# Two token groups run side by side under a static list schedule: an eight-core hybrid decoder step

## The chip, the cores and the metric

The kernel runs on all 8 cores of one Trainium2 chip (cores 0 to 3 are die 0, cores 4 to 7 die 1). Each core takes one prompt sequence and 16 decode sequences, and no core talks to another. The time is device microseconds (us) of the slowest core. PE is the matmul engine, ACT the scalar engine, DVE the vector engine, POOL the GpSimd engine, and SP the engine that only issues transfers here.

The runs fall in two states. In the fast one the two dies agree (kernel before: clocks of 0.92 to 0.95 on every core, and the dies' median spans within 0.7%); in the slow one the cores of one die show a lower granted PE clock and the time is longer.

## The reference, cut to what matters

Two layers; each token's activations `x` are 1024 wide. This is one layer:

```python
hn = rmsnorm(x, norm_in)
u_a, b_a, c_a, g_a, x_b, g_b, m_a, m_b = split(hn @ w_in)      # 8 x 1024 columns
y_a = b_a * conv3(c_a * u_a) * silu(g_a)                       # branch A
xc  = conv4(x_b) + bias                                        # branch B
r, gi = sigmoid(xc @ w_r), sigmoid(xc @ w_i)                   # block-diagonal, 64 x 64
a = exp(-8 * r * softplus(-lam))
h[t] = a[t] * h[t-1] + sqrt(1 - a[t]**2) * gi[t] * xc[t]       # scan over time
y_b = h * silu(g_b)
m = sigmoid(m_a) * (y_a @ w_a_out) + sigmoid(m_b) * (y_b @ w_b_out)
x = x + m @ w_o
x = x + (p @ w_pe) * sigmoid(rmsnorm(x, norm_pe) @ w_pg)
```

A final RMSNorm follows the second layer. Per core there are 2112 token columns: 2048 of the prompt and 64 of the decode group. The convolutions and the scan run along time, so a tile of columns needs the last few columns of the tile before it.

Below, the **A phase** of a token group is everything up to `y_a` and `y_b`; it is heavy on ACT and DVE (77% and 84% busy in the first row of the stretches below). The **B phase** is the merge, `w_o`, the second norm and the gate; it is mostly PE (100% in the second row, with ACT at 17% and DVE at 32%).

## The kernel before

Features lie on the 128 partitions and tokens on the free dimension. The tokens are handled as two groups, one wholly after the other, since the kernel's on-chip arrays hold `x`, `hn`, `ya`, `yb` and `mg` of one group at a time:

```python
def tiles_of(g):
    if g == 0:
        return [("p", 512, 0, 0), ("m", 512, 512, 512)]
    return [("p", 384, 0, 1024), ("p", 384, 384, 1408), ("p", 320, 768, 1792)]
...
for g in range(2):
    # load x of this group
    for l in range(L):
        norm_phase(g, V_NIN + l * 8, hn)
        for j in range(KC):                      # the A phase, 8 column blocks
            for ti, tile in enumerate(tl):
                c = ab_front(ui, g, l, j, ti, tile)
                if pend is not None:
                    ab_back(pend)                # gates and scan, one unit late
                pend = c
        ab_back(pend)
        # the B phase: mg_unit, wo_unit, norm_phase, gt_unit, each for 8 blocks
    norm_phase(g, V_NF, None, final=True, after_tile=store_tile)
```

Each engine's instruction stream is in program order, with semaphore waits computed from reads and writes. Weights are fetched by POOL into a ring of five slots, one 1024 x 128 column block per transfer:

```python
def wsrc_cols(wl, c0):
    return wl[:, c0:c0 + 128].rearrange("(k p) n -> p k n", p=128)
```

The sources are fp32, so that reads runs of 128 x 4 = 512 bytes; they are cast to bf16 on the way. SiLU is written with Tanh, the function that the sigmoids use as well, plus one vector instruction; the factors 0.5 are folded into other instructions:

```python
act(s2[:, 0:n], psum[b_gb][:, 0:n], AF.Tanh, [("ps", b_gb)], [s2k], scale=0.5)
...
stt(s2[:, 0:n], s2[:, 0:n], 1.0, psum[b_gb][:, 0:n], ALU.add, ALU.mult, [s2k, ("ps", b_gb)], [s2k])
```

## Time and profile before

The median of the first three runs is 1877.32 us, but two of these three are slow (1877.32 and 1899.26); the fast one is 1824.2. The profiled execution is a fast one with a span of 1819.5 us.

From the page of the kernel before: busy time and share of the span by engine; then the span in 40 slices, with a digit for tenths busy; then the weight queue (packets, MB, share of the 16 DMA engines' time); then the engines' shares in the chain that ended last; then one costly group (busy us, mean ns, idle time ahead of it).

```profile
PE 1565.0 (86%) x8200; PEld 809.0 (44%) x8200; DVE 1148.9 (63%) x2162; ACT 969.6 (53%) x1677; POOL 596.5 (33%) x715
...
PE   3989889988999889987198888999889889799985
...
PEclk9999999988999999988599999999889999999987
...
q0 software_dynamic: 415008, 105.48, 65.2%
...
PE 44%; DVE 22%; ACT 15%; issue 8%; DMA 7%; POOL 3%; DVEq 0%; ACTq 0%; POOLq 0%; SPq 0%
...
L226 ACT ACT_TABLE_LOAD x177 | 227.1, 1283 | 11.3 <-PE ps L250 7.2
```

PE is the busiest engine, but 1819.5 - 1565.0 = 254.5 us of the span it does nothing, and it makes up only 44% of the chain. The digits show where: many 8s, and a hole (7, 1) in the middle, where the first group ends and the second has to be loaded. The clock digits fall with it, to 5 (0.50 in the fourth row below).

Busy time by stretch says what each stage is worth. The columns are the stretch, its length, then busy time (and instructions) of PE, PEld, DVE, ACT and POOL, then granted clock, DMA share and GB/s.

```profile
75.00:264.00 189.00, 165.64 (x737) 71.63 (x736) 158.69 (x293) 144.63 (x227) 88.84 (x111) 0.97 0.74 64
264.00:376.00 112.00, 112.00 (x521) 50.67 (x520) 35.85 (x52) 18.63 (x31) 23.27 (x28) 1.00 0.74 66
376.00:440.00 64.00, 56.71 (x237) 23.32 (x236) 37.46 (x56) 22.26 (x37) 23.55 (x29) 0.92 0.75 67
860.00:912.00 52.00, 10.63 (x28) 3.12 (x29) 12.38 (x22) 12.84 (x30) 0.00 (x0) 0.50 0.88 192
```

The first row is an A phase: 737 matmuls in 189 us, 256 ns each, with DVE busy 84% and ACT 77%. The second is a merge: 521 matmuls in 112 us, 215 ns each, with DVE a third busy and ACT a sixth. So in one stage the vector work holds PE up, and in the next PE holds the others up. The fourth row is the hole between the groups.

The waits of PE name the same places (total us, times, longest):

```profile
PE ps L365 <- ACT wk_sq L226: 92.1, 21, 38.8
PE ps L250 <- DVE wk_xc L240: 81.3, 44, 3.0
PE ps L250 <- DMA wslot<-w_in: 17.4, 6, 7.2
```

The first is the norms (PE sums squares that ACT makes), with a single wait of 38.8 us between the groups. The second is the A phase. PE hardly ever waits for weights, though their queue takes 65% of the DMA engines.

### The profile page before, as it was taken

The numbers are of one execution on the slowest core, as the hardware profiler recorded it, in microseconds if no ns is written. First come the engines' busy times: TensorE is split into PE (matmuls) and PEld (weight loads), VectorE is DVE, ScalarE is ACT, GpSimd is POOL, SyncE is SP. The second block draws the span as 40 slices with busy tenths as digits, with TensorE's granted clock in tenths as the row PEclk, the third lists the DMA queues.
The fourth block names the chain that finished last, engine by engine and source line by source line (L and its number), as shares of the span: only waits on it lengthen the run. The fifth ranks groups of instructions, "written<-read, shape, count | busy, mean of one in ns | idle before, by whom it ended". The sixth has DMA issues, their size and how long they took to land.

```text
span 1819.5 us, 23966 instructions; the slowest of 8 cores (1808.0 to 1819.5 us)
## 1 busy us (share of the span) xinstructions
PE 1565.0 (86%) x8200; PEld 809.0 (44%) x8200; DVE 1148.9 (63%) x2162; ACT 969.6 (53%) x1677; POOL 596.5 (33%) x715
## 2 busy tenths in 40 slices
PE   3989889988999889987198888999889889799985
PEld 0333334433433334432054555566445445466642
DVE  3688872346888863356188888433678888833365
ACT  3577761134687751134278888411357888831144
POOL 5244451024345451023023444411233435340120
PEclk9999999988999999988599999999889999999987
DMA  9866979169676889269825739863594465894353
GB/s 171 81 50 56 79 66 103 18 60 86 60 63 53 75 72 97 25 59 97 203 20 51 69 37 90 72 60 30 54 101 39 43 63 51 77 90 44 38 52 117
DMA packets 426390, 126.05 MB, mean 69 GB/s; under 512 B 412832, under 2 KB 421792, under 8 KB 426272
## 3 DMA queue, kind: packets, MB, share of 16 engines
q0 software_dynamic: 415008, 105.48, 65.2%
q1 hardware_dynamic: 11264, 19.04, 3.6%
q8 instruction: 70, 1.15, 0.2%
q14 instruction: 48, 0.39, 0.1%
HBM read 220.44 MB, written 9.49 MB: 126 GB/s over the span
## 4 chain that ended last, share of the span: by engine, by line
PE 44%; DVE 22%; ACT 15%; issue 8%; DMA 7%; POOL 3%; DVEq 0%; ACTq 0%; POOLq 0%; SPq 0%
PE ps L250 42%; DVE wk_xc L240 9%; ACT wk_th L226 5%; DMA wslot<-w_in 5%; DVE wk_h L533 4%; DVE wk_ti L229 2%; PE ps L365 2%; ACT wk_a L226 2%; DVE x L240 2%; ACT wk_ti L226 1%; ACT wk_tr L226 1%; DMA yT<-x 1%; DVE hn L240 1%; DVE wk_tg L240 1%; ACT wk_xc L226 1%
## 5 line engine op out<-in xcount | busy, mean ns | idle before, releaser
L250 PE MATMUL ps<-hn,wslot 128*128 128x512 bf16 (+2 forms) x5760 | 1119.3, 350 | 115.5 <-DVE wk_xc L240 81.3
L250 PEld LDWEIGHTS ps<-hn,wslot 128*128 128x128 bf16 x5760 | 568.8, 100 | 624.3 <-issue 189.1
L226 ACT ACTIVATE wk_tg<-ps 128x512 f32<-128x512 f32 (+2 forms) x240 | 125.0, 521 | 281.8 <-PE ps L250 199.0
L315 POOL DMA_DIRECT2D wslot<-w_in x256 | 228.8, 908 | 119.7 <-PE ps L250 100.9
L240 DVE SCALAR_TENSOR_TENSOR wk_tg<-wk_tg,ps 128x512 f32<-128x512 f32 (+2 forms) x240 | 141.8, 591 | 157.1 <-PE ps L250 114.2
L226 ACT ACT_TABLE_LOAD x177 | 227.1, 1283 | 11.3 <-PE ps L250 7.2
L229 POOL TENSOR_TENSOR ya<-wk_cv,wk_tg 128x512 bf16<-128x512 f32 (+2 forms) x80 | 106.9, 1336 | 342.8 <-DVE wk_cv L240 342.8
L226 ACT ACTIVATE wk_sq<-x 128x512 bf16<-128x512 f32 (+2 forms) x200 | 93.2, 541 | 162.3 <-PE ps L365 75.4
L226 ACT ACTIVATE wk_cv<-ps 128x320 f32<-128x320 f32 (+1 forms) x160 | 83.3, 521 | 179.5 <-PE ps L250 179.5
L365 PE MATMUL ps<-wk_sq,ones 128*128 128x512 bf16 (+2 forms) x200 | 81.8, 461 | 106.9 <-ACT wk_sq L226 92.1
L240 DVE SCALAR_TENSOR_TENSOR wk_xc<-ps,vecs_sb,wk_xc 128x511 f32<-128x511 f32 (+8 forms) x240 | 152.6, 636 | 9.9 <-ACT sop_sb L419 3.9
L240 DVE SCALAR_TENSOR_TENSOR hn<-x,vecs_sb,wk_xc 128x512 bf16<-128x512 f32 (+2 forms) x160 | 92.9, 652 | 92.2 <-ACT wk_xc L226 92.2
L240 DVE SCALAR_TENSOR_TENSOR wk_cv<-wk_cv,ps 128x512 f32<-128x512 f32 (+2 forms) x80 | 47.5, 594 | 163.8 <-PE ps L250 163.8
L250 PE MATMUL ps<-ya,wslot 128*128 128x512 bf16 (+2 forms) x640 | 130.3, 347 | 0.0
L250 PE MATMUL ps<-yb,wslot 128*128 128x512 bf16 (+2 forms) x640 | 127.3, 342 | 2.9 <-POOL yb L229 2.9
L315 POOL DMA_DIRECT2D wslot<-w_o x32 | 28.1, 877 | 289.9 <-PE ps L250 289.9
L229 POOL TENSOR_TENSOR yb<-wk_h,wk_s 128x512 bf16<-128x512 f32 (+2 forms) x80 | 86.4, 1080 | 108.2 <-DVE wk_h L533 108.2
L229 DVE TENSOR_TENSOR wk_ti<-wk_th,wk_ti 128x512 f32<-128x512 f32 (+2 forms) x80 | 57.7, 721 | 93.1 <-ACT wk_th L226 93.1
L250 PE MATMUL ps<-mg,wslot 128*128 128x512 bf16 (+2 forms) x640 | 115.0, 342 | 0.0
L240 DVE SCALAR_TENSOR_TENSOR wk_cv<-wk_cu,dv,wk_cv 128x384 f32<-128x384 f32 (+3 forms) x160 | 102.4, 640 | 2.8
L365 PEld LDWEIGHTS ps<-wk_sq,ones 128*128 128x128 bf16 x200 | 20.4, 102 | 167.2 <-issue 165.9
L226 ACT ACTIVATE wk_th<-wk_th 128x512 f32<-128x512 f32 (+2 forms) x160 | 88.8, 555 | 3.4
(71 smaller groups left out, 1487.6 us busy)
## 6 DMA issues: line engine op xcount, KB each, us to landing
wslot<-w_in POOLq DMA_DIRECT2D x256, 256.0 KB, 11.4
wslot<-w_a_out POOLq DMA_DIRECT2D x32, 256.0 KB, 14.4
wslot<-w_b_out POOLq DMA_DIRECT2D x32, 256.0 KB, 17.7
wslot<-w_o POOLq DMA_DIRECT2D x32, 256.0 KB, 4.5
wslot<-w_pg POOLq DMA_DIRECT2D x32, 256.0 KB, 4.5
x<-xin SPq DMA_DIRECT2D x2, 2048.0 KB, 20.1
yT<-x SPq DMA_DIRECT2D x2, 2048.0 KB, 23.4
x<-xin SPq DMA_DIRECT2D x2, 1536.0 KB, 14.4
```

Source lines behind the costliest of these rows:

```text
L226: P.op("act", lambda e: e.activation(out=out, in_=in_, func=func, **kw), reads, writes)
L229: P.op(eng, lambda e: e.tensor_tensor(out=out, in0=in0, in1=in1, op=op), reads, writes)
L240: P.op("dve", lambda e: e.scalar_tensor_tensor(out=out, in0=in0, scalar=scalar, in1=in1, op0=op0, op1=op1), reads, writes)
L250: ins = e.matmul(out=psum[bk][:, 0:n], lhsT=lh, rhs=rh, start=(i == 0), stop=(i == len(pairs) - 1))
L315: pending.append((ui_, (lambda e, s=src, d=dst: e.dma_start(out=d, in_=s)), first))
L365: return e.matmul(out=psum[bk][:, 0:n], lhsT=ones[:], rhs=sq[:, 0:n], start=(k == 0), stop=(k == KC - 1))
L533: P.op("dve", lambda e: e.tensor_tensor_scan(out=h[:, 0:n], data0=a_[:, 0:n], data1=ti_[:, 0:n], initial=init_ap, op0=ALU.mult, op1=ALU.ad ...
```

## The change

The intent: PE should always have work that doesn't depend on what ACT and DVE are doing. The A phase of one group is run beside the B phase of the other, five stages in all: A(g0) alone, then B(g0) with A(g1), B(g1) with A(g0) of layer 2, B(g0) with A(g1), and B(g1) alone. To make room for both groups, fixed arrays give way to 82 equal buffers that are handed out and taken back, and `x` is written to DRAM between the layers. The whole program is first recorded as a graph of operations with estimated durations; a list scheduler then fixes the order of each engine's instructions. Some details change as well: SiLU is one ACT function, tiles are 424 columns (one is 416), the last columns of a tile are copied into the head of the next tile's buffer, and weights are laid out on the host in the order in which a transfer writes them. The number of matmuls and their total columns stay the same.

The diff, cut to its core:

```diff
+TN = (424, 424, 424, 424, 416)
+GROUPS = ((0, 1), (2, 3, 4))
+NBUF = 82                                  # arena of 128 x 428 fp32 buffers
+class Graph:                               # ops with durations, priorities, reads, writes
+    SETS = {"tanh": ("exp", "silu"), "exp": ("exp", "lnexp"), "silu": ("silu",), ...}
+    def schedule(self):
+        while n_left:
+            for e in ENG:                   # for each engine, its best ready op
+                for o in cand[e]:
+                    ...                     # must have buffers, PSUM banks and ring slots
+                    key = o.prio
+                    if e == "act" and o.aset and cur[0] not in self.SETS[o.aset]:
+                        key += 4.0          # prefer what the loaded table can do
+                    k2 = (max(s - T, 0.0) > 0.02, s if s > T + 0.02 else 0.0, key, o.idx)
+            ...                             # issue the earliest one

-w_in = din("w_in", [L, D, INC])
+w_A = din("w_A", [L, KC, 3, 128, 2048])    # and w_M, w_O, w_G: rows of 8192, 4096, 5120 bytes
...
-                pending.append((ui_, (lambda e, s=src, d=dst: e.dma_start(out=d, in_=s)), first))
+            fn = lambda e: e.dma_start(out=ring[v.phys][:, 0:cols], in_=src)

-            act(tg[:, 0:n], psum[b_ga][:, 0:n], AF.Tanh, [("ps", b_ga)], [tgk], scale=0.5)
-            stt(tg[:, 0:n], tg[:, 0:n], 1.0, psum[b_ga][:, 0:n], ALU.add, ALU.mult, ...)
+            G2(1.5, [("act", d_act(n))], lambda e, en: e.activation(
+                out=f32(tg, 0, n), in_=ps(bga, 0, n), func=AF.Silu), [bga], [tg], aset="silu")

+        stage_len = [ucols(0) * PER_COL * 1.05]
+        stage_len += [(ucols(0) + ucols(1)) * PER_COL * 1.02] * 3
+        stage_len += [ucols(1) * PER_COL]
+        def a_phase(l, g, hns):
+            G.stream = 0
+            S, Ln = stage_t[2 * l + g], stage_len[2 * l + g]
+        def b_phase(l, g, hns, ya, yb):
+            G.stream = 1
+            s = 2 * l + g + 1               # beside the A phase of the next stage
+            ...
+                    if l == 0:
+                        nxt[g, ti] = norm(t, xs[ti], V_NIN + 8, pr)
+                        store_x(t, xs[ti], xsp, pr, True)     # x spilled to DRAM
```

## The prediction

> **What bounds it now.** The profiled run (fast state, span 1819.5 us, both dies at clock 0.94) is limited by TensorE, imperfectly: the page has PE 1565 us busy (86%), DVE 1149, ACT 970, POOL 597. In the stretches table the merge/output stages (273 to 364 us, 1592 to 1729) are dense: 423 matmuls of 512 columns in 91 us, 215 ns each, granted clock 1.00 on all eight cores. So 8200 matmuls of 422.4 columns on average need about 8200 x 177 ns = 1450 us. The other 370 us are idle time (255) and matmuls at a reduced clock (about 110).
>
> Where they lie (stretches, timeline):
> - start: the first projection matmul at 32.6 us, then 7 us waiting for weights;
> - A/B phases (75 to 264): 189 us for 737 matmuls worth 158 us; PE waits for wk_xc, the chain runs through DVE, ACT and POOL;
> - norms (376 to 440: PE 57 of 64 us, clock 0.92);
> - group change (860 to 912): PE busy 10.6 of 52 us at clock 0.50, waiting for the x load and its squares;
> - end, about 30 us.
>
> **What the change does.** Matmul columns stay the same. The A phase of one group is interleaved with the B phase of the other, so PE always has independent work; group change and inner norms disappear as PE stalls. Weights come as contiguous rows instead of 512 B packets (412832 of 426390 packets are under 512 B; queue 0 takes 65% of the DMA engines). Spilling x adds about 26 MB to 220 MB of HBM reads: harmless.
>
> Costs: summed from trace durations, interpolated to 424 columns, DVE stays near 1165 us (silu saves 160 STTs of 0.59 us, but merges, ya, yb and some squares go from POOL to DVE). ACT needs about 680 us of ACTIVATEs plus, by walking the new instruction order, about 330 table loads (177 before) at 1.283 us = 420 us. [...] the trace shows the next ACTIVATE 20 ns after the load[...]. Both engines fill about 70 to 75% of the new span and should hide under PE, except in the first A phase, which runs alone: ACT about 10 us per unit, PE 8.9.
>
> **Sum (fast state).** 1450 PE + start 16 + first A phase 20 + tail 30 + 4% stalls of a static order (50) [...] = about 1575.
>
> Slow state: two of three runs before were 3 to 4% slow. [...] the fast trace shows 1.00 for 137 dense us on all cores, so I don't expect it throughout, but a denser kernel should [...] lose 6 to 8% then, having less slack. Weighing both: **1600 us, range 1540 to 1710**; faster by over 2%: 0.94, within 2%: 0.04, slower: 0.02.
>
> **Right if:** PE busy share is 94% or more; no slice but the first and last is below 8 tenths; clock 0.97 or more in a fast run; PE over 75% of the chain; the 39 us wait for wk_sq gone; DMA share below 50%; table loads about 420 us.
>
> **Wrong if:** [...] ACT or DVE stall PE through PSUM banks (1650 to 1700, PE waits naming them); POOL's halo copies delay DVE.

The sum came to about 1575 us. The terms left in it add to 1450 + 16 + 20 + 30 + 50 = 1566; one of 10 us is cut, since no trace gave its figure. Apart from the 1450, the terms are estimates. The 6 to 8% of the slow state are the author's estimate beside the 3 to 4% of the two slow runs before; neither they nor the 25 us from 1575 to 1600 are derived further.

## The result and the profile after

The changed kernel is correct and takes 1611.61 us (median of five runs: 1607.88, 1611.57, 1611.61 and 1615.35 fast, 1859.74 slow). The ratio of the mean time of its fast runs to that of the fast runs of the kernel before of the same rounds is 0.883, with a 95% interval of 0.8795 to 0.8866. (All ratios here are made that way, so they are not quite the ratios of the medians that are quoted.) The prediction was 1600 us in 1540 to 1710.

The page of the kernel after, the same parts:

```profile
PE 1499.3 (93%) x8200; PEld 807.0 (50%) x8200; DVE 1095.8 (68%) x1960; ACT 1039.4 (65%) x1522; POOL 346.9 (22%) x724
...
PE   2989869999999999999999998999999999999984
...
PEclk9999989999999999999999999999999999999997
...
q0 software_dynamic: 39200, 105.46, 39.1%
...
PE 74%; ACT 11%; DVE 7%; DMA 4%; issue 3%; POOL 1%; SPq 1%; DVEq 0%; POOLq 0%; ACTq 0%
```

The profiled span fell by 1819.5 - 1606.3 = 213.2 us. PE's idle time fell from 254.5 to 107.0 us, which is 147.5 of them. PE's busy time fell by the other 65.7 us for the same 8200 matmuls, while the mean granted clock rose from 0.94 to 0.98.

The stretches of the kernel after, same columns as before; the rows are the start, the first A phase, the three mixed stages, the last B phase and the tail:

```profile
0.00:36.00 36.00, 11.59 (x32) 3.53 (x32) 4.70 (x9) 17.12 (x26) 13.82 (x32) 1.00 1.02 186
36.00:241.00 205.00, 169.50 (x858) 86.87 (x859) 154.86 (x316) 160.38 (x237) 57.47 (x148) 0.92 0.48 92
241.00:1365.00 1124.00, 1106.52 (x6154) 602.32 (x6153) 823.95 (x1443) 793.25 (x1135) 256.63 (x512) 0.99 0.47 91
1365.00:1526.00 161.00, 157.59 (x870) 85.72 (x868) 54.54 (x93) 34.18 (x64) 13.78 (x25) 0.98 0.55 109
1526.00:1606.00 80.00, 54.06 (x291) 28.54 (x288) 57.74 (x103) 34.51 (x60) 5.19 (x7) 0.86 0.32 87
```

In the mixed stages PE is busy 98% of the time and runs a matmul every 1124/6154 = 183 ns. ACT and DVE are busy there 71% and 73%, as evenly as hoped. What is left is at the ends: the first A phase still has nothing to run beside, and its 858 matmuls take 239 ns each.

PE's waits after:

```profile
PE ps L528 <- ACT buf L522: 31.4, 13, 10.4
PE ps L556 <- DVE buf L544: 10.5, 3, 4.2
PE ps L556 <- DMA wa<-w_A: 9.3, 7, 3.4
PE ps L556 <- DVE dv L465: 8.1, 1, 8.1
```

Both big waits of before are gone: the 38.8 us one between the groups, and the 81.3 us for the conv result. The first row is again the norms, but 20.9 of its 31.4 us lie in the first 36 us, where there is nothing else to do.

One slow run is on record for this kernel: 1859.74 us with die 1 at a clock of 0.813 to 0.827, 15% over the fast runs. Slow runs of the kernel before, over all rounds, were 2 to 9% over its fast ones.

### Lag: a sum that can be checked

A matmul of 424 columns takes 177 ns in the dense stretches (227 in 40.2 us), so at any time the lag is that time minus 177 ns for each matmul done so far. This is the mean over the 8 cores of the lag at the end of each stretch:

| kernel | 36 us | 241 us | 1365 us | 1526 us |
|---|---|---|---|---|
| after | 30.3 | 81.0 | 115.6 | 121.5 |
| no table loads (experiment 3) | 30.3 | 69.0 | 99.3 | 106.9 |
| Silu undone (experiment 4) | 30.3 | 72.1 | 91.4 | 98.9 |

The lag at the end of the kernel after is about 148 us (the mean span of its cores, 1599.3 us, less 8200 times 177 ns). So the start costs 30 us, the first A phase another 51, the three mixed stages 35 in all, and the last B phase with the tail 32.

### The profile page after: what moved, and what is told of

Read it like the earlier page. It is cut to its first block, busy times and chain, and to the rows that moved or that the text cites. A ratio compares the mean times of both kernels' runs of the same rounds, so it can differ in the third digit from the quotient of the medians.

```text
span 1606.3 us, 23920 instructions; the slowest of 8 cores (1594.1 to 1606.3 us)
## 1 busy us (share of the span) xinstructions
PE 1499.3 (93%) x8200; PEld 807.0 (50%) x8200; DVE 1095.8 (68%) x1960; ACT 1039.4 (65%) x1522; POOL 346.9 (22%) x724
## 4 chain that ended last, share of the span: by engine, by line
PE 74%; ACT 11%; DVE 7%; DMA 4%; issue 3%; POOL 1%; SPq 1%; DVEq 0%; POOLq 0%; ACTq 0%
PE ps L556 72%; DVE buf L544 2%; DMA wa<-w_A 2%; ACT L715 1%; PE ps L528 1%; DMA wb<-w_M 1%; DMA buf<-xin 1%; DVE buf L540 1%; PE ps L699 1%; ACT buf L715 1%; ACT buf L713 1%; ACT L711 1%; ACT buf L711 1%; SPq L507 1%; PE ps L702 1%
## 5 line engine op out<-in xcount | busy, mean ns | idle before, releaser
L556 PE MATMUL ps<-buf,wb 128*128 128x424 bf16 (+1 forms) x4000 | 748.1, 345 | 25.2 <-DVE dv L465 8.1
L556 PE MATMUL ps<-buf,wa 128*128 128x424 bf16 (+1 forms) x3840 | 729.4, 346 | 32.1 <-DMA wa<-w_A 9.3
L556 PEld LDWEIGHTS ps<-buf,wb 128*128 128x128 bf16 x4000 | 393.5, 99 | 357.9 <-issue 42.2
L556 PEld LDWEIGHTS ps<-buf,wa 128*128 128x128 bf16 x3840 | 378.4, 99 | 355.1 <-issue 54.9
L792 DVE SCALAR_TENSOR_TENSOR buf<-buf,ps 128x424 f32<-128x424 f32 (+1 forms) x160 | 94.4, 592 | 197.0 <-PE ps L556 157.3
L790 ACT ACTIVATE buf<-ps 128x424 f32<-128x424 f32 (+1 forms) x160 | 81.8, 520 | 163.8 <-PE ps L556 159.8
L624 DVE SCALAR_TENSOR_TENSOR buf<-buf,vecs_sb 128x424 f32<-128x424 f32 (+2 forms) x240 | 156.1, 651 | 4.4 <-ACT buf L615 2.2
L544 DVE SCALAR_TENSOR_TENSOR buf<-buf,vecs_sb 128x424 bf16<-128x424 f32 (+1 forms) x160 | 99.5, 693 | 36.4 <-ACT buf L534 36.4
L522 ACT ACTIVATE buf<-buf 128x424 bf16<-128x424 f32 (+1 forms) x108 | 58.9, 553 | 84.8 <-DVE buf L808 41.0
L680 DVE SCALAR_TENSOR_TENSOR buf<-buf,vecs_sb 128x424 f32<-128x424 f32 (+2 forms) x160 | 108.4, 678 | 2.0
L715 ACT ACT_TABLE_LOAD x80 | 102.6, 1283 | 1.4
L528 PE MATMUL ps<-buf,ones 128*128 128x424 bf16 (+1 forms) x200 | 54.2, 356 | 32.1 <-ACT buf L522 31.4
L746 ACT ACTIVATE buf<-ps 128x424 f32<-128x424 f32 (+1 forms) x80 | 41.9, 523 | 54.3 <-PE ps L556 52.1
L829 ACT ACTIVATE buf<-ps 128x424 f32<-128x424 f32 (+1 forms) x80 | 41.2, 520 | 54.2 <-PE ps L556 41.3
L599 ACT ACTIVATE buf<-ps 128x360 f32<-128x360 f32 (+2 forms) x80 | 40.4, 505 | 53.5 <-PE ps L556 53.4
L711 ACT ACT_TABLE_LOAD x57 | 73.1, 1283 | 1.0
L649 ACT ACTIVATE buf<-ps 128x360 f32<-128x360 f32 (+2 forms) x80 | 40.7, 509 | 47.0 <-PE ps L556 46.1
L689 ACT ACT_TABLE_LOAD x48 | 61.6, 1283 | 11.9 <-PE ps L556 11.2
```

What stands on the lines that cost most here:

```text
L522: return e.activation(out=b16(h, a, a + n), in_=f32(x, 0, n), func=AF.Square)
L528: G.op([("pe", d_mm(n, 1))], lambda e, en, h=h, a=a, k=k: e.matmul(out=ps(bk, 0, n), lhsT=ones[:], rhs=b16(h, a, a + n), start=(k == 0), s ...
L544: G.op([("dve", d_sttp(n))], lambda e, en, x=xs[k], h=h, a=a, k=k: e.scalar_tensor_tensor(out=b16(h, a, a + n), in0=f32(x, 0, n), scalar=v ...
L556: ins = e.matmul(out=ps(bk, 0, n), lhsT=ring[w.phys][:, off + k * 128:off + (k + 1) * 128], rhs=b16(src[k // 2], a, a + n), start=(k == 0) ...
L624: G2(0.1 + 0.01 * d, [("dve", d_sttp(npr))], lambda e, en, d=d: e.scalar_tensor_tensor(out=f32(xc, 0, npr), in0=f32(xb, 3 - d, 3 - d + npr ...
L680: G2(1.3 + 0.01 * d, [("dve", d_sttp(npr))], lambda e, en, d=d: e.scalar_tensor_tensor(out=f32(cv, 0, npr), in0=f32(cu, d, d + npr), scala ...
```

## The experiments

Twelve kernels ran, three timed rounds each beside the kernel before. Four questions guided them: how much the interleaving is worth, what the ACT table loads cost, what the weight layout is worth, and what could shorten the start. "Theory" and "rival" are those of the quoted expectations.

### 1. The changed kernel again

No edit; it gives the later runs a reference on another chip.

> The changed kernel unaltered, as the yardstick for the other runs of this chip: 1605 to 1620 us in the fast state, first A phase (36 to 241 us) about 205 us long, about 304 table loads. If a slow execution comes up it should be near 1850 us, since nearly all of its time is matmul time and the slow die's clock is about 0.82.

1612.19 us, ratio 0.8851 (0.8814 to 0.8888), all four runs fast, mean 1611.4. The result stands.

### 2. Interleaving undone

The same scheduler, arena, tiles, Silu and weights, but all operations are one stream with eight stages one after another.

```diff
-        stage_len = [ucols(0) * PER_COL * 1.05]
-        stage_len += [(ucols(0) + ucols(1)) * PER_COL * 1.02] * 3
-        stage_len += [ucols(1) * PER_COL]
+        stage_len = [ucols((i // 2) % 2) * PER_COL * 1.05 for i in range(8)]
...
-            G.stream = 1                    # in b_phase
-            s = 2 * l + g + 1
+            G.stream = 0
+            s = 4 * l + 2 * g + 1
```

> Only the interleaving is undone: all operations in one stream, eight stages one after another, scheduler, buffers, Silu and weight layout kept. Theory 1 (the gain is the overlap of A with B): the four A phases take about 205 us (16 units) and 290 us (24 units) as the first one does now, the B phases stay at PE speed, in all 1720 to 1790 us, so most of the gain over before is lost. Rival (the gain is list scheduling, spare buffers and earlier loads, that close the gaps at norms, group change and weights): 1620 to 1660 us.

1757.59 us, ratio 0.9654 (0.9595 to 0.9713), fast mean 1756.3. So the interleaving seemed worth 1756 - 1611 = 145 us, most of the gain, as the theory had it. The stretch of an A phase in this order (columns as above) shows what came back:

```profile
438.00:613.00 175.00, 155.00 (x847) 80.63 (x846) 130.10 (x225) 160.66 (x216) 46.43 (x90) 1.00 0.30 51
```

ACT is busy 160.66 of 175 us, 92%, while PE falls to 89%. That points to ACT, not DVE, as what binds this A phase. It made the table loads the next suspect (57 of them take 73 us of this stretch), and experiment 6 had to correct the reading of this one.

### 3. The same order without the table loads

To take the loads away and leave everything else where it is, Silu became Tanh and Sqrt became Exp in the emitted instructions only; the scheduler still saw the old functions, and the instruction order is the same on every engine. The results are wrong on purpose.

```diff
-... func=AF.Silu), [bga], [tg], aset="silu")
+... func=AF.Tanh), [bga], [tg], aset="silu")
-... func=AF.Sqrt, bias=dcol(DV_QTR), scale=-0.25), [tr, st_dv], [tr], aset="sqrt")
+... func=AF.Exp, bias=dcol(DV_QTR), scale=-0.25), [tr, st_dv], [tr], aset="sqrt")
```

> Wrong results on purpose: Silu becomes Tanh and Sqrt becomes Exp, so that all functions but the norms' Ln lie in one table set; the order of the instructions on every engine is the same, nearly all of the 304 table loads go. Theory (the first A phase is bound by ScalarE, of whose 205 us some 75 are loads): the first A phase falls to 160 to 170 us and the whole to about 1560 to 1570 us, the middle three stages gain under 15 us. Rival (the first A phase is bound by weight landings, PSUM turn-around or DVE): the whole stays within 10 us of the changed kernel.

1587.44 us, ratio 0.8726 (0.869 to 0.8763), fast mean 1588.7. Table loads (summed over all lines of ACT) fell from 310 to 33, of which 16 come at a logarithm (15 of them in the norms), and 277 x 1.283 = 355 us of ACT time with them, but the kernel gained only 23 us. That lies between the theory (45) and the rival (under 10); the theory was too large. The lag table says where: the first A phase shortened by 12 us and the mixed stages together by 4 (34.6 to 30.3). Something else binds that phase too, and this run does not say what; PE's waits in it are spread over weights and norms. (The 8 us that the profile puts down to `dv`, small constants, end as DVE finishes the second tile's norm: in the kernel after it is at the norm from 35.96 to 40.62 us, and PE starts at 40.76.)

### 4. Silu undone

Here the function is taken back for real, and the scheduler builds its own order around it. It gives correct results.

```diff
-            G2(1.5, ... func=AF.Silu), [bga], [tg], aset="silu")
+            G2(1.5, ... func=AF.Tanh, scale=0.5), [bga], [tg], aset="tanh")
+            G2(1.55, [("dve", d_stt(n))], lambda e, en: e.scalar_tensor_tensor(
+                out=f32(tg, 0, n), in0=f32(tg, 0, n), scalar=1.0, in1=ps(bga, 0, n), op0=ALU.add, op1=ALU.mult), [bga, tg], [tg])
             # and likewise for g_b; the later product takes the factor 0.5
```

> Silu is undone: tanh of half the argument and a scalar_tensor_tensor instead, 160 more of these on VectorE (about 95 us), and the table loads fall from 304 to about 200. Theory (PE bound in the middle, ScalarE bound at the start): the middle is unchanged, the first A phase is shorter by 5 to 20 us, the whole 1590 to 1610 us. Rival (VectorE, at 68% of the span, already costs time): slower than the changed kernel by 10 us or more.

1589.95 us (median of six, of which two are slow), ratio 0.8713 (0.867 to 0.8756), fast mean 1586.3. One part of the change is thus a loss of about 25 us: without it the kernel is faster. The loads fall from 310 to 190, far fewer than experiment 3 took away, and the gain is as large. The lag table shows why: the mixed stages lag by 91.4 - 72.1 = 19 us here, against 35 in the kernel after and 30 in experiment 3. The simplest reading is that with fewer functions that exclude each other the scheduler finds an order with fewer stalls, and that this is worth more there than the load time itself. This is argued and not shown: between experiments 3 and 4 the order differs, but so does the work (33 and 190 loads, more vector instructions in the second), and no run changes the order alone. The chain of this kernel:

```profile
PE 79%; DMA 7%; DVE 5%; ACT 4%; issue 3%; POOL 1%; SPq 0%; DVEq 0%; POOLq 0%; ACTq 0%
```

ACT's share fell from 11% to 4%.

### 5. Silu alone, in the kernel before

```diff
-            act(tg[:, 0:n], psum[b_ga][:, 0:n], AF.Tanh, [("ps", b_ga)], [tgk], scale=0.5)
+            act(tg[:, 0:n], psum[b_ga][:, 0:n], AF.Silu, [("ps", b_ga)], [tgk])
-            stt(tg[:, 0:n], tg[:, 0:n], 1.0, psum[b_ga][:, 0:n], ALU.add, ALU.mult, ...)
             # and likewise for s2; the factors 0.5 folded elsewhere become 1.0
```

> Only Silu is done, in the kernel before: 160 scalar_tensor_tensors less on VectorE (about 95 us), one more table load per tile on ScalarE (about 80 more, 100 us). Theory (Silu was part of the gain because VectorE is on the chain of the A/B phases): ratio 0.97 to 0.985. Rival (the loads put back on ScalarE, as much on the chain, eat it): ratio 0.99 to 1.02.

1914.19 us, ratio 1.0523 (1.0486 to 1.056): slower by 96 us, more than either expectation allowed. The groups and PE's waits of this kernel:

```profile
L226 ACT ACT_TABLE_LOAD x253 | 324.6, 1283 | 9.5 <-PE ps L250 4.0 <-PEq L121 1.1
...
PE ps L250 <- DVE wk_xc L240: 134.0, 53, 4.2
```

There are 76 more loads, 97.5 us of ACT time, and PE's wait for the conv result grows by 53 us. The wait is an upper bound: this trace lacks 65 of the 8200 matmuls, and a missing one counts as idle time. The 160 vector instructions that Silu saves (0.59 us each) bought nothing there.

### 6. Silu and the interleaving both undone

The edits are those of experiments 2 and 4 together.

> Interleaving and Silu undone together. In the serial run ScalarE was 90% or more busy in the A phases, a third of it table loads; in the changed kernel undoing Silu gave 22 us. Theory (what the overlap hides is ScalarE's time in the A phases, and Silu makes it longer there): Silu undone gives three or more times as much without the overlap, 1660 to 1690 us against 1757. Rival (serial is slow for boundaries and weight waits, not for ScalarE): it gives 25 us or less, 1730 us or more.

(Measured in the serial run, experiment 2: ACT busy 160.15 of 205 us, 78%, in the first A phase and 92% in the stretch shown there, with table loads 73 of its 160.66 us, 45%; over the whole span 301 loads are 386 of the 1047 us that ACT is busy, 37%.)

1667.7 us, ratio 0.9124 (0.9092 to 0.9156), fast mean 1666.6. So without overlap Silu costs 1756.3 - 1666.6 = 90 us, against 25 us with it, and once Silu is out, the interleaving is worth 1666.6 - 1586.3 = 80 us, not 145. (This kernel ran on another chip than the other two; by the ratios, which allow for that, it is 96 and 75 us.) The A phase from 438 to 613 us, as shown for experiment 2, is now

```profile
438.00:613.00 175.00, 170.29 (x951) 92.41 (x949) 161.30 (x282) 157.25 (x237) 54.91 (x93) 1.00 0.31 55
```

with PE at 97% though nothing runs beside it. The 145 us of experiment 2 were in part damage from Silu that the interleaving hides.

### 7. The weight layout alone undone

The tensors are the reference's own, read in runs of 512 bytes into the same ring slots; the order on PE, ACT, DVE and SP is the same, instruction for instruction.

```diff
-            fn = lambda e: e.dma_start(out=ring[v.phys][:, 0:cols], in_=src)
+            for wl, c0, kk in src:
+                fns.append(lambda e, wl=wl, c0=c0, kk=kk, off=off: e.dma_start(
+                    out=ring[v.phys][:, off:off + kk * 128].rearrange("p (k n) -> p k n", n=128),
+                    in_=wl[:, c0:c0 + 128].rearrange("(k p) n -> p k n", p=128)))
+                off += kk * 128
```

> Only the weight layout is undone: the changed kernel reads the weights from their first layout in rows of 512 B (two transfers of 256 KB instead of one of 512 KB); PE, ACT, DVE and SP carry the same instructions in the same order. Theory (weights are loaded far enough ahead, the layout only lowers the load of the DMA engines): DMA share of the weight queue back from 39% to 65 to 75%, time within 1% of the changed kernel, 1610 to 1628 us, the loss in the start and the first A phase. Rival (the weight queue paces the denser kernel): 2% or more slower, 1645 us or over, with PE waits for wa and wb all over the span.

1721.78 us, ratio 0.9425 (0.9368 to 0.9483), fast mean 1716.0: 105 us slower than the kernel after. My theory (within 1%) fell and the rival stands. The queue, PE's longest waits for weights and the landing time of the A-phase weights (KB each, us from issue to landing) in this kernel:

```profile
q0 software_dynamic: 415008, 105.48, 65.6%
...
PE ps L564 <- DMA wa<-w_in: 69.0, 25, 6.4
...
PE ps L564 <- DMA wb<-w_a_out: 16.1, 3, 7.9
...
wa<-w_in POOLq DMA_DIRECT2D x192, 256.0 KB, 7.2
```

and the landing time in the kernel after:

```profile
wa<-w_A POOLq DMA_DIRECT2D x96, 512.0 KB, 7.0
```

For the same 105 MB the queue takes 0.656 x 1720.9 = 1129 us of each DMA engine's time here and 0.391 x 1606.3 = 628 us in the kernel after: 1.8 times as long. On the profiled cores PE's waits for weights are 95 us here and 16 there, but these are the worst core of the one and the best of the other: the means over the 8 cores are 70 and 24 us, so that weights account for 46 of the 82 us by which the mean span of the profiled cores grew (1599 to 1681); where the other 36 come from stays open. A transfer of half the size lands no sooner (7.2 us against 7.0). The cores also differ more (spans 1657 to 1721 us, against 1594 to 1606 in the kernel after), though their programs are the same, and the slowest of them sets the 105 us. In this kernel 415,872 of the 444,791 packets are counted under 512 bytes (512 bytes of fp32 arrive as 256 of bf16: 105.48 MB in 415,008 packets).

### 8. The layout kept, the transfers halved

Experiment 7 changed two things, the length of the rows and the number of transfers. Here each transfer of more than 1024 columns is cut in two, so that there are as many issues as in experiment 7, with rows of 4 KB.

```diff
-            fn = lambda e: e.dma_start(out=ring[v.phys][:, 0:cols], in_=src)
+            h = 1024 if cols > 1024 else cols
+            fns = [lambda e, a=a: e.dma_start(out=ring[v.phys][:, a:min(a + h, cols)], in_=src[:, a:min(a + h, cols)])
+                   for a in range(0, cols, h)]
```

> The changed kernel with each weight transfer cut into pieces of 256 KB with 4 KB rows: as many transfers and as many issues on POOL as with the 512 B rows, but few rows. PE, ACT, DVE and SP carry the same instructions in the same order. rows512 was 105 us slower than the changed kernel. Theory (the DMA engines' time per short row made it slow: 65% mean share, waits for wa and wb): halves stays within 8 us of the changed kernel, 1605 to 1620 us. Rival (twice the issues and completions [...] made it slow): half or more of the loss comes back, 1660 us or more.

1643.37 us (two of five runs are slow), ratio 0.8979 (0.8937 to 0.902). Against 0.883 and 0.8851 for the kernel after that is 23 to 27 us more, about a quarter of the 105 us. So the count and size of the transfers cost a quarter at most, and the rest comes from the short rows. It is at most, since the rows were halved as well, from 8 KB to 4 KB. This too lies between theory and rival. In the profile of this kernel:

```profile
q0 software_dynamic: 66848, 105.48, 42.5%
...
PE ps L558 <- DMA wa<-w_A: 38.6, 16, 6.8
```

The queue's time is only 0.425 x 1641.8 = 698 us, so here it is probably not the DMA engines' load that PE waits for, but when the pieces land. In all, 256 KB against 512 KB, with rows of half the length, cost some 25 us here.

### 9. The layout alone, in the kernel before

The same transfers, slots and order; only the source tensors are blocked on the host.

```diff
         def wsrc_cols(wl, c0):
-            return wl[:, c0:c0 + 128].rearrange("(k p) n -> p k n", p=128)
+            return wl[c0 // 128]
```

> Only the weight layout is done, in the kernel before: contiguous 4 KB per partition and block. Theory (only the start waited for weights): 5 to 25 us faster than before, ratio 0.985 to 0.998, PE wait for wslot falls from 17 us to under 5. Rival (the layout carries a good part of the gain): ratio 0.97 or less.

Five of six runs fell into the slow state; the one fast run is 1794.2 us, 25 us (1.4%) under the mean of the fast runs before (1819.5), and no ratio can be given for one run. The cores of undisturbed dies settle it all the same, since no core waits for another. In the fast run and in four of the slow ones, at least one die kept a clock of 0.94 to 0.95: these 24 core spans are 1785 to 1794 us, mean 1789.9, and all lie below the 52 of the undisturbed dies of the kernel before in the same rounds (1802 to 1826, mean 1811.4). The gain is 21 to 22 us (1.2%), as the theory had it, far below the 105 us of experiment 7, and PE's waits for weights, 2 to 17 us on the cores of the kernel before, are gone on every core. The queue's line in this kernel, beside 65.2% before:

```profile
q0 software_dynamic: 66848, 105.48, 38.9%
```

### 10. Interleaving, Silu and layout all undone

The edits are those of experiments 2, 4 and 7 together. What is left is the list schedule, the arena and the five nearly equal tiles.

> Interleaving, Silu and the weight layout all undone: what remains of the change is the list scheduling, the arena and five nearly equal tiles. serial_tanh took 1665 us in the fast state, before 1820 to 1830. In the kernel before the layout was worth 1.5% (one fast run, 27 us), in the interleaved kernel 105 us. Theory (the layout is worth little where the kernel has slack): 1685 to 1715 us. Rival (list-scheduled streams have no slack for late weights, interleaved or not): 1740 us or more, so that scheduling alone is worth under 90 us.

1759.04 us, ratio 0.9693 (0.9625 to 0.976), fast mean 1760.9. The rival was right: the layout is worth 1760.9 - 1666.6 = 94 us in this order as well (104 by the ratios), so its worth hardly depends on the interleaving. PE's waits for weights have a mean over the cores of 103 us here and 49 in experiment 6. The largest of them, on the profiled cores of this kernel and then of experiment 6:

```profile
PE ps L562 <- DMA wa<-w_in: 61.5, 30, 16.1
```

```profile
PE ps L554 <- DMA wa<-w_A: 32.5, 18, 18.2
```

The worth of the layout depends on which of the two programs it is in. A likely reason is that the kernel before issues a load as soon as a slot is free, while the scheduler issues it by a priority some 20 us ahead of its modelled need, with a modelled rate that is the same for both layouts. No run separates this: a scheduler told a slower rate for the short rows might lose less.

### 11 and 12. The start

The lag is 30 us at the start, so I tried to let `x` come in ahead of all else: first the block-diagonal gate weights as two padded transfers after the first `x` tile (experiment 11), then, with Silu undone, the first weights too behind the sixth piece of `x` and a slower modelled rate for the first loads (experiment 12).

```diff
-                        fns.append(lambda e, s=src, d=dst: e.dma_start(out=d, in_=s))
-                G.op([("pool", 3.0)], fns, [], [v], PR, ...)
+                G.op([("pool", 0.6)], [lambda e, s=wsrc, d=dst: e.dma_start(out=d, in_=s)], [X00[-1]], [v], PR, ...)
```

> A mend of the start of the changed kernel: the two gate matrices come block-diagonal and zero-padded from DRAM as two transfers with 8 KB rows, issued after the first x tile has landed, instead of 8 transfers with 256 B rows ahead of it. Theory (the first 21 us wait for x pieces that share the DMA engines with 4096 short rows): the first projection matmul comes at 16 to 22 us instead of 28.5, the whole is 6 to 12 us shorter than the changed kernel. Rival (x is slow because the pieces are issued one by one at 0.86 us each from one queue): under 4 us shorter.

Experiment 12 adds, besides the edit of experiment 4:

```diff
-            R = [prev_load[kind]] if prev_load[kind] is not None else []
+            R = [prev_load[kind]] if prev_load[kind] is not None else [XW[0]]     # XW[0]: the sixth piece of x
...
-                     ..., dma=("buf", n * 512 / 330e3, v, res))
+                     ..., dma=("buf", n * 512 / (150e3 if res == 0 else 330e3), v, res))
```

> The best run so far (tanh, about 1585 us) with a start in another order: the first weights wait for six of the eight pieces of the first x tile, the gate matrices come as two padded transfers after that tile, and the scheduler reckons with 150 GB/s for the first x tiles. The run start showed that the x pieces, not the gates, set the time (about 190 GB/s in the first 36 us). Theory (the first tile's bytes were shared with 2 MB of weights): first projection matmul at 18 to 24 us, the whole 6 to 15 us under tanh, 1570 to 1580 us. Rival (the weights come too late in exchange): within 4 us of tanh or slower.

Experiment 11: 1612.61 us, ratio 0.8898 (0.8819 to 0.8976), no gain. The first projection matmul comes at 26.5 us instead of 28.5, not at 16 to 22. The rival's number was right; its cause, issues of 0.86 us each (13.73 us for 16 pieces in the trace of the kernel after), was not, since the first three pieces land 4 to 5 us apart. These are ACT's squares of the second and third piece, on the profiled core of the kernel after and then of experiment 11 (start us, duration, instruction, idle time before it and what ended it):

```profile
10.97 0.56 ACT L522 ACTIVATE buf<-buf 128x424 bf16<-128x424 f32 x1 [5.30 <-DMA buf<-xin]
15.15 0.56 ACT L522 ACTIVATE buf<-buf 128x424 bf16<-128x424 f32 x1 [3.62 <-DMA buf<-xin]
```

```profile
10.94 0.56 ACT L516 ACTIVATE buf<-buf 128x424 bf16<-128x424 f32 x1 [4.58 <-DMA buf<-xin]
14.58 0.56 ACT L516 ACTIVATE buf<-buf 128x424 bf16<-128x424 f32 x1 [3.08 <-DMA buf<-xin]
```

Moving the gate weights out of the way brought the third piece 0.6 us forward, and PE then waited for the second tile's norm instead. In both, about 190 GB/s reach the profiled core in the first 36 us (186 and 193), while all eight load.

Experiment 12: the fast runs are 1582.87 and 1585.52 us, ratio 0.8674 (0.8638 to 0.871). Its trace shows what held the pieces up. With the first weights kept back they land one or two us apart, as ACT's squares show (second piece, then third to fifth), but the first projection then waits for its weights:

```profile
6.75 0.56 ACT L517 ACTIVATE buf<-buf 128x424 bf16<-128x424 f32 x1 [0.57 <-DMA buf<-xin]
8.73 1.59 ACT L517 ACTIVATE buf<-buf 128x424 bf16<-128x424 f32 x3 [1.43 <-DMA buf<-xin]
```

```profile
22.20 2.99 PE L551 MATMUL ps<-buf,wb 128*128 128x424 bf16 x8 [8.75 <-DMA wb<-w_M]
```

So the theory was right that `x` shared the DMA engines with the weights, and the first projection comes within its 18 to 24 us (28.3 in experiment 4). It bought nothing: PE then waits for the second tile's norm until 40.0 us (41.0 in experiment 4). The fast mean of 1584.2 us is the lowest, but its interval overlaps that of experiment 4 (0.8713), as the rival had it, and two of its four runs were slow (1835.57 and 1866.73). That it beats experiment 4 is not shown; that both beat the kernel after is.

## Where the time came from

From the fast runs, one step after the other; the differences of ratios are multiplied by 1820 us, a round mean of the fast runs before:

| step | kernel | ratio | change by ratios, us | change of fast means, us |
|---|---|---|---|---|
| before | | 1 | | |
| list schedule, arena, five tiles and all else | experiment 10 | 0.9693 | -56 | -57 |
| weight layout | experiment 6 | 0.9124 | -104 | -94 |
| interleaving | experiment 4 | 0.8713 | -75 | -80 |
| Silu | experiment 1 | 0.8851 | +25 | +25 |

The kernels ran on three chips, each beside the kernel before, so the ratios are the safer column. The order of the steps matters: with Silu in, the interleaving is worth 145 us. But in no order is it the whole of the gain, and in no kernel tried here did Silu pay: it cost 96 us in the kernel before, 90 to 96 in the serial order and 25 in the interleaved one.

## Why the prediction was right or wrong

The total was right: 1600 us predicted (1575 for a fast run), 1611.61 measured, inside the range, and faster as said. The reasons held up less well than the number. All fast runs took about 1611 us, 36 more than the 1575 that the sum gave for them; 25 of these 36 were covered by what had been added for slow runs, and the median is that of a fast run. Of the 36, 22 lie in the terms below and about 12 are the time of the slowest core over the mean span of the cores, which the sum left out.

**Right.** PE's dense time of 8200 x 177 ns = 1450 us was the floor, and the mean span of the cores came within 148 us of it. The 39 us wait for squares between the groups is gone. The clock is 0.98. The weight queue fell to 39%. That the slow state would not last throughout was right as well: the fast runs granted a mean clock of 0.97 to 0.99 to all eight cores over 1600 us, and only a die of the one slow run ran at 0.81 to 0.83.

**Mis-sized terms.** The prediction's sum was 1450 + start 16 + first A phase 20 + static order 50 + tail 30, and the 10 of the term that is cut. Measured by lag (which includes the time at a lower granted clock): start 30, first A phase 51, mixed stages 35, end 32. The start and the first A phase were 45 us too small together, the stalls of the static order 15 too large. "ACT about 10 us per unit, PE 8.9" was the step behind the 20 us: it took the first A phase to be bound by one engine working without gaps. Experiment 3 showed that even without the loads it lags by 39 us, so most of its loss is in waits shared out over several causes. Three of the marks were missed by a little for this reason: PE share 93% (94 or more predicted) and 74% of the chain (over 75), and one slice inside the first A phase has 6 tenths.

**Silu.** The prediction counted it as a saving of 160 vector instructions, with more table loads that "should hide under PE". They do not hide: 310 loads took 398 us (330 loads and 420 us predicted, so the count was good), and undoing Silu gained 25 us. Silu drives the loads from 190 to 310 (from 177 to 253 in the kernel before) and cost time in each of the three pairs of kernels. The step that failed is that ACT and DVE, at 70 to 75% of the span, "should hide under PE, except in the first A phase". ACT was busy even less, 65%, yet by the lag table 15 of the roughly 25 us that undoing Silu gained lie in the mixed stages, and only 9 in the first A phase. In the mixed stages nearly all the loads together cost only 4 us (experiment 3); that the rest is the order, with fewer good choices when functions are split among more tables, is likely but not shown. What was said of a single load was right: 1283 ns is the mean of every group of loads in the traces, and in the lines below, from ACT's timeline of the kernel before, the next function starts 20 ns after the load ends, and the load 10 ns after the function before it.

```profile
148.12 0.63 ACT L226 ACTIVATE wk_th<-wk_th 128x512 f32<-128x512 f32 x1
148.76 1.28 ACT L226 ACT_TABLE_LOAD   x1
150.06 0.63 ACT L226 ACTIVATE wk_th<-wk_th 128x512 f32<-128x512 f32 x1
```

**The weight layout.** The prediction mentioned it as fewer packets and gave it no time, since PE waited only 17.4 us for weights before. It is worth about 100 us. What the prediction missed is that slack in the old program doesn't carry over to the new one: in the old one the old rows cost 22 us, in the new one PE waits 55 to 95 us for them, by core.

**Interleaving.** It was named as the main cause. Beside a kernel with all other parts of the change it is worth 145 us, beside one without Silu 80. The mechanism was right (PE at 98% in the mixed stages), the size depends on the company it keeps. That the mis-sized terms partly cancelled (45 us too small against 25 too large, the 10 of the cut term among these), and that the allowance for slow runs covered most of the rest, was luck.

**The slow state.** Predicted: 6 to 8% lost, an estimate. The one slow run of the kernel after lost 15%. That a denser kernel meets this state more often is not shown: 1 of 9 runs of the kernel after was slow, 4 of 10 of the two Silu-free ones of experiments 4 and 12, and 10 of 33 of the kernel before; experiment 9, no denser than that, had 5 of 6.

**Still open:** what else binds the first A phase besides the table loads; whether the short rows hurt through the landing times alone or also through POOL, whose issue takes 0.91 us with them (0.55 in experiment 8); and why the same rows cost 22 us in the old program and 105 in the new.

## What to carry to other kernels

Phases bound by different engines are worth running side by side, but undo each companion of such a change by itself: here one part that rode along (Silu) was a loss that the overlap hid, and another that looked like housekeeping (rows of 4 to 8 KB in transfer order instead of 512 bytes) was worth as much as the overlap itself, about 100 us, though it is worth only 22 in the old program. An activation function that brings more table loads should be judged by the number of loads in the trace (190 without Silu, 310 with it) and by the stage where its engine is on the chain, not by the vector instructions that it saves or the engine's mean share. And a wait that is short in the old order says little of the wait in a new one (17.4 us for weights before, 55 to 95 us for the same rows in experiment 7): after a reschedule, cost each transfer anew. When runs fall in the slow state, the cores of an undisturbed die can still answer the question (mean spans of 1789.9 against 1811.4 us in experiment 9), where the cores don't wait for one another.
